# A conditioned decoder layer: loads in program order, scale and norm in one operation, remainder from the first part, quarter sums later

## The chip, the core and the metric

The kernel runs on one NeuronCore of a Trainium2 chip. The metric is the device time of one execution in microseconds, which is to be small. The core has a matrix engine (TensorE, PE in the profile; its weight loads are PEld), a vector engine (VectorE, DVE), an activation engine (ScalarE, ACT), GpSimd (POOL) and SyncE (SP), which here only issues transfers. Each runs its own instructions in order and waits on semaphores for the others. Transfers (DMA) are issued from the queues of SP, ACT and POOL.

## What is computed

One decoder layer over 2048 tokens of width 1024, and a final norm. Cut to what matters here:

```python
mod = c @ w_ada + b_ada                       # adaLN: shift, scale, gate
shift, scale, gate = split(mod, 3)
h = rmsnorm(x, g_pre) * (1.0 + scale) + shift
p = h @ w_in                                  # eight blocks of 1024 columns
y_a = conformer_conv_branch(p[A value], p[A glu], p[A silu], ...)   # conv of width 31
v = layernorm(gelu(p[B v]))                   # v: the block that the kernel takes first
s = tril(w_s) v + b_s                         # per head, in chunks of 128 positions
y_b = (gelu(p[B u]) * s * silu(p[B silu])) @ w_out_b
x = x + gate * ((sigmoid(p[gA]) * y_a + sigmoid(p[gB]) * y_b) @ w_o)
out = rmsnorm(x, g_final)
```

## The kernel before

All matrices are fp32. For the matrix engine each operand is split into two parts of type fp32r: the first part (`hi`) is a rounded copy made by ScalarE, the remainder (`lo`) is the value minus that copy. A product of two split operands is three matmuls: hi·hi, hi·lo and lo·hi. `split` (L84) does this for weights: ScalarE copies (L87), VectorE or GpSimd subtracts (L88).

The tokens are worked in two stages of 1024 (`s` = 0, 1), and a stage in two halves of 512. A stage first makes h, transposed: eight tiles `xn[k]` of 128 channels, of which `A[h][k]` are the split copies. Then it makes the v block (`first`, `v_pass`), its Gelu and layer norm (`v_half`, `v_norm`), and the position mixing per head (`mixing`, whose results `r` are stored to memory by GpSimd's queue). Then 28 steps called `quad` follow: each makes a 2x2 block product with seven products in place of eight, out of quarter sums `S1` to `S4` of h and sums of weight quarters. The convolution runs on VectorE beside them as background work. The output projections follow.

The change concerns the stretch before the first `quad` of stage 0, and in a smaller part the first `quad` of each stage:

- **The opening.** The first half of `xt` (x transposed) is loaded (L471), squared on ScalarE (L491, L494) and summed on VectorE (L495). `col_sums` and `spread` turn that into `rx`, the reciprocal norm of each token on all partitions. The row of c (`crow`) is loaded and spread over the partitions by two matmuls into `cbc` (L483, L486).
- **The first pass** is a loop of eight steps over k (L527). A step makes the adaLN columns of channel tile k + 1 (`ada`, L398: two reductions of 128x1024 weights `wa` against `cbc`, then an addition), scales `xn` by `rx` (`scaled`, L503), makes h twice on ScalarE by the Identity of scale times value plus shift (`shifted`, L507, through `modulated`, L364: once into the first part, once in place), and subtracts them for the remainder (L529). It splits two weight pieces of `w_v` by `prep_to` (L538). The matrix engine does 24 matmuls a step: 16 with the first part of h (L552, L553), 8 with the remainder (L557). The last step (L562 on) goes by output tile, so that tiles can be evicted one by one.
- **The norm of the second half** is taken from the second half of `xn`: squares (L545) in steps 4 to 7, sums (L560), `col_sums`, then `spread` and `make_h` (L369).
- **The quarter sums** (`halves_sums`, L378) are made for stage 0 and 1 at L633, and split into `S1` at once, into `S2`, `S4` and `S3` after the layer norm of the second half (`after`, L648).

The order within an engine is that of the program text inside `tc.manual_schedule(engines=MANUAL)` (L475), where MANUAL is PE, DVE, ACT and POOL. SP is not in it: a scheduler orders its loads, there and everywhere else, and all engines after the block. Pools bound how far a load may run ahead: 8 tiles `raw` for weights as loaded, 5 tiles `whl` for split pieces, 28 tiles `hs` for h, adaLN weights, v and sums, 6 small tiles `t512` (`r`, `rx` and others), 6 banks of PSUM.

## Time and profile before

| | us |
|---|---|
| median of the runs before (3 runs) | 1917.8 |
| lowest and highest run | 1916.1 and 1923.04 |
| the profiled execution | 1916.63 |
| its span in the trace | 1914.7 |

The profile page of that execution gives the matrix engine 96% busy, VectorE 70%, ACT 45% and POOL 46%. Of its forty slices of the span, the first, of some 48 us, has PE at 60%, the second at 70%, the third at 90% and nearly all others at 80% or more. A busy PE counts the modelled length of its matmuls, and the clock that it was granted is a figure of its own (1.00 is full speed, 2.4 GHz; 0.50 is 1.2 GHz). Times inside the trace run from the start of the span. Of a row of the timeline the first number is the start, the second the length; a count xN means N instructions merged into one row; in brackets stands how long the engine sat idle before, and who ended that.

### The profile page before, as it was taken

Reading aid. Unit: us, or ns where it says so; the run is one execution under the profiler, and the core shown is the slowest. Engines: PE = TensorE matmul, PEld = TensorE weight load, DVE = VectorE, ACT = ScalarE, POOL = GpSimd, SP = SyncE. Lnnn points to the kernel's source line nnn. Section 1 sums busy time; section 2 is a strip of 40 time slices with the busy share of each in tenths; the row PEclk is TensorE's granted clock in tenths of the full one; section 3 lists DMA queues with packets and bytes.
Section 4 is the critical chain, followed back from the end, with each engine's and each line's share of the span. In section 5 each row is a group of like instructions: output and inputs, shape, how many; then the busy total and the mean of one; then the engine's idle time right before and its main releaser. Section 6 shows DMA issues by size and latency. Waiting matters only on the chain.

```text
span 1914.7 us, 23225 instructions
## 1 busy us (share of the span) xinstructions
PE 1846.7 (96%) x8116; PEld 1507.4 (79%) x8116; DVE 1332.7 (70%) x1636; ACT 862.5 (45%) x1394; POOL 873.8 (46%) x734
## 2 busy tenths in 40 slices
PE   6798999999999999989999989999999998999998
PEld 4577888888888778778888878888888887888886
DVE  6775988888988874365851578789887798634424
ACT  4545555555455662312611454545554556512102
POOL 0035777777777740100100477777777776110000
PEclk9799999999999999999999999999999999999999
DMA  9562332223332368775886331333222333954494
GB/s 332 182 242 94 105 116 94 94 83 116 105 116 83 108 246 283 250 262 189 339 309 215 125 138 67 115 105 116 100 100 74 113 121 113 344 181 138 131 341 171
DMA packets 139015, 313.66 MB, mean 164 GB/s; under 512 B 15889, under 2 KB 16017, under 8 KB 138898
## 3 DMA queue, kind: packets, MB, share of 16 engines
q1 hardware_dynamic: 108434, 237.03, 36.5%
q0 software_dynamic: 11888, 41.43, 5.6%
q10 hardware_dynamic: 18576, 33.73, 4.6%
q8 instruction: 63, 1.03, 0.2%
q14 instruction: 54, 0.44, 0.1%
HBM read 226.66 MB, written 85.46 MB: 163 GB/s over the span
## 4 chain that ended last, share of the span: by engine, by line
PE 75%; issue 9%; DVE 6%; DMA 5%; ACT 3%; POOL 2%; SPq 0%; ACTq 0%; POOLq 0%; DVEq 0%
PE bank L297 21%; PE bank L303 21%; PE bank L300 21%; PE bank L312 3%; PE bank L313 3%; PE bank L314 3%; DVE a L892 1%; DMA raw<-in_wgate 1%; DVE wa L400 1%; PE bank L439 1%; DMA wa<-in_wada 1%; POOL whl L88 1%; DMA xn<-in_xt 1%; DMA whl<-d_wo 1%; ACT whl L87 1%
## 5 line engine op out<-in xcount | busy, mean ns | idle before, releaser
L88 POOL TENSOR_TENSOR whl<-raw,whl 128x512 fp32r<-128x512 f32 x392 | 520.9, 1333 | 348.5 <-ACT whl L87 344.0
L717 DVE SCALAR_TENSOR_TENSOR cv<-a,vec,cv 128x1024 f32<-128x1024 f32 x464 | 596.6, 1286 | 31.6 <-ACT cv L711 21.4
L87 ACT ACTIVATE whl<-raw 128x512 fp32r<-128x512 f32 x504 | 314.1, 626 | 405.8 <-PE bank L303 221.6
L300 PE MATMUL bank<-s,whl 128*128 128x512 f32 x896 | 350.2, 391 | 3.0 <-DVE s L88 3.0
L303 PE MATMUL bank<-s,whl 128*128 128x512 f32 x896 | 351.6, 392 | 0.0
L297 PE MATMUL bank<-s,whl 128*128 128x512 f32 x896 | 350.9, 392 | 0.0
L224 POOL TENSOR_TENSOR raw<-raw 128x512 f32<-128x512 f32 x224 | 295.8, 1321 | 17.2
L297 PE MATMUL bank<-h,whl 128*128 128x512 f32 x672 | 264.0, 393 | 0.5 <-DVE snap L693 0.4
L300 PE MATMUL bank<-h,whl 128*128 128x512 f32 x672 | 262.5, 391 | 0.0
L303 PE MATMUL bank<-h,whl 128*128 128x512 f32 x672 | 261.6, 389 | 0.0
L300 PEld LDWEIGHTS bank<-s,whl 128*128 128x128 f32 x896 | 168.9, 188 | 40.7 <-DVE s L88 5.1
L297 PEld LDWEIGHTS bank<-s,whl 128*128 128x128 f32 x896 | 169.0, 189 | 36.1 <-issue 1.2
L303 PEld LDWEIGHTS bank<-s,whl 128*128 128x128 f32 x896 | 169.0, 189 | 35.4 <-issue 0.8
L297 PEld LDWEIGHTS bank<-h,whl 128*128 128x128 f32 x672 | 126.1, 188 | 33.2 <-DVE snap L693 6.6
L303 PEld LDWEIGHTS bank<-h,whl 128*128 128x128 f32 x672 | 126.1, 188 | 26.8 <-issue 0.5
L300 PEld LDWEIGHTS bank<-h,whl 128*128 128x128 f32 x672 | 126.2, 188 | 26.0 <-issue 0.5
L88 DVE TENSOR_TENSOR whl<-raw,whl 128x512 fp32r<-128x512 f32 x112 | 76.0, 688 | 52.0 <-ACT whl L87 49.5
L921 POOL DMA_DIRECT2D mb<-gl x32 | 17.3, 541 | 201.3 <-DVE gl L920 201.3
L665 ACT ACTIVATE snap<-bank 128x512 f32<-128x512 f32 x112 | 66.5, 597 | 90.8 <-PE bank L303 90.8
L303 PE MATMUL bank<-ya,whl 128*128 128x512 f32 x256 | 100.6, 393 | 6.7 <-DVE whl L88 6.6
L297 PE MATMUL bank<-ya,whl 128*128 128x512 f32 x256 | 100.4, 392 | 0.5 <-ACT whl L87 0.5
L297 PE MATMUL bank<-yb,whl 128*128 128x512 f32 x256 | 99.8, 390 | 0.9 <-ACT whl L87 0.9
(218 smaller groups left out, 2882.2 us busy)
## 6 DMA issues: line engine op xcount, KB each, us to landing
raw<-in_w_in SPq DMA_DIRECT2D x224, 256.0 KB, 3.0
yb<-yb SPq DMA_DIRECT2D x32, 512.0 KB, 7.8
whl<-d_wo SPq DMA_DIRECT2D x32, 512.0 KB, 4.3
whl<-d_wv SPq DMA_DIRECT2D x32, 512.0 KB, 4.2
xn<-in_xt SPq DMA_DIRECT2D x32, 256.0 KB, 5.5
wa<-in_wada SPq DMA_DIRECT2D x16, 512.0 KB, 6.5
raw<-in_w_v SPq DMA_DIRECT2D x32, 256.0 KB, 4.8
d_wv<-whl POOLq DMA_DIRECT2D x16, 512.0 KB, 6.3
```

Of the source, the lines that this page charges most:

```text
L87: nc.scalar.activation(hi, val, AF.Copy)
L88: eng.tensor_tensor(out=lo, in0=val, in1=hi.bitcast(F32), op=ALU.subtract)
L224: eng.tensor_tensor(out=dst, in0=dst, in1=src, op=ALU.add)
L297: nc.tensor.matmul(pt, wh, h[:, 0], start=start and k == 0, stop=False, skip_group_check=True)
L300: nc.tensor.matmul(pt, wh, h[:, 1], start=False, stop=False, skip_group_check=True)
L303: nc.tensor.matmul(pt, wl, h[:, 0], start=False, stop=k == last, skip_group_check=True)
L312: nc.tensor.matmul(pt, xh, w[:, 0], start=kt == 0, stop=False)
L313: nc.tensor.matmul(pt, xh, w[:, 1], start=False, stop=False)
L314: nc.tensor.matmul(pt, xl, w[:, 0], start=False, stop=kt == KT - 1)
L400: nc.vector.tensor_tensor_reduce(out=wa[i], in0=wa[i], in1=cbc, scale=col(V_GPRE, k) if i else 1.0, scalar=0.0, op0=ALU.mult, op1=ALU.add, ...
L665: nc.scalar.activation(t, pt, AF.Copy)
L717: nc.vector.scalar_tensor_tensor(out=dst, in0=a[:, k : k + S], scalar=col(V_CW, j * TAPS + k), in1=cv[0], op0=ALU.mult, op1=ALU.add,)
```

## The change

1. SP joins the manual schedule of the block. The first half of `xn` is loaded by two queues, even tiles on SP and odd ones on ACT. `vec` (the small columns) is loaded by ACT behind them, not first. `cbc` is loaded by a transfer that repeats the row of c over the partitions; `crow`, its two matmuls and its two copies go. Then come the loads of step 0 to 3 (`load_step`: two `wa`, two `raw` each), and in step k those of step k + 4. In step 3 four tiles `sx` of x itself (tokens on partitions) and the second half of `xn` are queued behind them.
2. A small Sqrt (`warm`) is the first work on ACT, and a small Gelu comes before the evictions.
3. `scaled` multiplies by rx and by the adaLN scale in one operation (scalar_tensor_tensor). ScalarE then only adds the shift: `h_hi` into the first part, `shifted` in place. The remainder `h_lo` is (value + shift) minus the first part, in one VectorE operation, and so no longer reads what `shifted` writes.
4. The order in a step: `ada`, `scaled`, `h_hi`, the split of two weight pieces, `h_lo`, `shifted`.
5. The norm of the second half comes from `sx`: four Squares with accumulation on ScalarE, in steps 5 and 6, in place of eight Squares and four sums. Its `spread` stands between tile 2 and tile 3 of the last step.
6. The quarter sums are made later: S1 after the layer norm of the second half, S2, S4 and S3 with `mixing(1)`, which itself moves in the first `quad` from behind the third product to ahead of it.

```diff
-    def spread(cols, pt=None):
+    def diagonal(cols):
...
+        return diag
+
+    def spread(cols, pt=None, diag=None):
+        diag = diagonal(cols) if diag is None else diag
...
-    def modulated(dst, src, k):
+    def scaled(xn, rx, h, k):
+        v = xn[k][:, h * T : (h + 1) * T]
+        nc.vector.scalar_tensor_tensor(
+            out=v, in0=v, scalar=mod[:, k, 1:2], in1=rx, op0=ALU.mult, op1=ALU.mult
+        )
+
+    def shifted(xn, h, k, dst=None):
+        v = xn[k][:, h * T : (h + 1) * T]
         nc.scalar.activation(
-            dst, src, AF.Identity, bias=mod[:, k, 0:1], scale=mod[:, k, 1:2]
+            v if dst is None else dst, v, AF.Identity, bias=mod[:, k, 0:1]
         )
 
+    def h_hi(xn, h, k, A):
+        A[h].append(hs("h"))
+        shifted(xn, h, k, A[h][k][:, 0])
+
+    def h_lo(xn, h, k, A):
+        t = A[h][k]
+        nc.vector.scalar_tensor_tensor(
+            out=t[:, 1], in0=xn[k][:, h * T : (h + 1) * T], scalar=mod[:, k, 0:1],
+            in1=t[:, 0].bitcast(F32), op0=ALU.add, op1=ALU.subtract,
+        )
...
-    with tc.manual_schedule(engines=MANUAL):
...
+    with tc.manual_schedule(engines=MANUAL | {ET.SP}):
+        warm = sm.tile([P, 8], F32, tag="cols", name="warm")[:, :1]
+        nc.scalar.activation(warm, eps_t, AF.Sqrt)
+        for k in range(KT):
+            (nc.scalar if k % 2 else nc.sync).dma_start(
+                out=xn[k][:, :T], in_=xt[k * P : (k + 1) * P, :T]
             )
-            nc.scalar.activation(cbc[:, n * T : (n + 1) * T], pt, AF.Copy)
+        nc.scalar.dma_start(out=vec, in_=vecs)
+        nc.sync.dma_start(out=cbc, in_=rows[:, 3 * D : 4 * D].broadcast_to([P, D]))
+
+        def load_step(k):
+            wa[k] = load_ada(k)
+            for n in range(2):
+                raw_row(w_v, k, n)
+
+        for k in range(4):
+            load_step(k)
...
         for k in range(KT):
...
+            if k + 4 < KT:
+                load_step(k + 4)
+            if k == 3:
+                for c in range(NC):
+                    sx.append(hs32("sx"))
+                    nc.sync.dma_start(out=sx[c], in_=x[T + c * P : T + (c + 1) * P, :])
+                load_xn(0, 1, xn)
             if k + 1 < KT:
-                wa[k + 1] = load_ada(k + 1)
-                scaled(k + 1)
                 ada(k + 1, wa[k + 1])
+                scaled(xn, rx, 0, k + 1)
+                h_hi(xn, 0, k + 1, A)
                 prep_to(2 * k + 4)
-                shifted(k + 1)
-            if k == 2:
-                load_xn(0, 1, xn)
-            if k >= 4:
-                sq.append(hs32("q"))
-                for i in range(2):
+                h_lo(xn, 0, k + 1, A)
+                shifted(xn, 0, k + 1)
+            if k in (5, 6):
+                for c in (2 * k - 10, 2 * k - 9):
                     nc.scalar.activation(
-                        sq[-1][:, i * T : (i + 1) * T], xn[2 * (k - 4) + i][:, T:S], AF.Square
+                        sx[c], sx[c], AF.Square, accum_out=ssx[:, c : c + 1]
                     )
...
+        c1 = rstd_cols(ssx, NC)
+        diag1 = diagonal(c1)
+        nc.scalar.activation(warm, eps_t, AF.Gelu)
...
-            if u < 2:
-                evict(u)
...
+            if u == 2:
+                evict(0)
+                evict(1)
+                nc.scalar.activation(rx1, spread(c1, None, diag1), AF.Copy)
+                scaled(xn, rx1, 1, 0)
...
-        sums4 = [halves_sums(xn, k) for k in range(KH)]
...
+        S1 = sum_group(sum1)
+        S2, S4, S3 = [], [], []
+
+        def mix_second():
+            mixing(1, vn1, wsT, sbias)
+            S2.extend(sum_group(sum2))
+            S4.extend(sum_group(sum4))
+            S3.extend(sum_group(sum3))
...
             run_bg(2)
+            if beside:
+                beside.pop()()
             c = bank()
             prod(c, [take()], S1)
...
-            if beside:
-                beside.pop()()
             prod(c, [take()], S4, start=False)
```

Three places show how the order on the engines moves. The first is VectorE in one step of the first pass (`whl` are the weight pieces, `h` the split copy of h, `ISA` the two reductions and the reading of their sums). Before:

```order
L404 TENSOR_TENSOR mod<-mod,base 128x2
L88 TENSOR_TENSOR whl<-raw,whl 128x512 x2
L529 TENSOR_TENSOR h<-xn,h 128x512
L505 TENSOR_TENSOR xn<-xn,rx 128x512
L400 ISA wa,mod<-wa,cbc 128x1024
```

VectorE in one step after the change:

```order
L439 TENSOR_TENSOR mod<-mod,base 128x2
L374 SCALAR_TENSOR_TENSOR xn<-xn,mod,rx 128x512
L88 TENSOR_TENSOR whl<-raw,whl 128x512 x2
L390 SCALAR_TENSOR_TENSOR h<-xn,mod,h 128x512
L434 ISA wa,mod<-wa,cbc 128x1024
```

The scaling has moved from ahead of the reductions to behind them, directly ahead of the two subtractions for the weights.

ACT in two steps before, from the end of step 0's preparation on (L87 copies weight pieces, L365 makes h):

```order
L87 ACTIVATE whl<-raw 128x512 x4
L365 ACTIVATE h<-xn,mod 128x512
L365 ACTIVATE xn<-xn,mod 128x512
L87 ACTIVATE whl<-raw 128x512 x2
L365 ACTIVATE h<-xn,mod 128x512
```

ACT at the same place after the change:

```order
L380 ACTIVATE xn<-xn,mod 128x512
L380 ACTIVATE h<-xn,mod 128x512
L87 ACTIVATE whl<-raw 128x512 x2
L380 ACTIVATE xn<-xn,mod 128x512
L380 ACTIVATE h<-xn,mod 128x512
```

Before, four weight pieces were copied ahead of the second h, so that the copies ran one step ahead of the subtractions; now the two copies of a step stand behind that step's h.

The second place is SP's queue of loads at the start. Before:

```order
L469 DMA crow<-in_rows 1x1024
L342 DMA xn<-in_xt 128x512 x8
L394 DMA wa<-in_wada 128x1024 x2
L174 DMA raw<-in_w_v 128x512 x8
L342 DMA xn<-in_xt 128x512 x7
L394 DMA wa<-in_wada 128x1024 x2
L342 DMA xn<-in_xt 128x512
L174 DMA raw<-in_w_v 128x512 x2
L580 DMA wsT<-in_wst 128x1024
L394 DMA wa<-in_wada 128x1024 x2
```

SP's queue after the change, from the same start (six more pairs of each kind follow up to step 7):

```order
L515 DMA xn<-in_xt 128x512 x4
L519 DMA cbc<-in_rows 128x1024
L429 DMA wa<-in_wada 128x1024 x2
L177 DMA raw<-in_w_v 128x512 x2
L429 DMA wa<-in_wada 128x1024 x2
L177 DMA raw<-in_w_v 128x512 x2
```

The second half of `xn` and `wsT` have moved from ahead of the adaLN weights of step 1 and 2 to behind all of step 7.

The third place is PE in the first `quad` of stage 0, around `mixing(1)` (rows with `vn`). Before:

```order
L297 MATMUL bank<-s_1249,whl 128x512
L300 MATMUL bank<-s_1249,whl 128x512
L303 MATMUL bank<-s_1249,whl 128x512
L439 MATMUL bank<-wsT,vn 128x128 x28
L297 MATMUL bank<-s_1253,whl 128x512
L300 MATMUL bank<-s_1253,whl 128x512
L439 MATMUL bank<-wsT,vn 128x128 x4
```

PE there after the change:

```order
L305 MATMUL bank<-h,whl 128x512
L308 MATMUL bank<-h,whl 128x512
L311 MATMUL bank<-h,whl 128x512
L478 MATMUL bank<-wsT,vn 128x128 x32
L305 MATMUL bank<-s,whl 128x512
L308 MATMUL bank<-s,whl 128x512
L311 MATMUL bank<-s,whl 128x512
```

The 32 matmuls of the mixing have moved from behind the products with S1 and S2 to directly behind the two products with h, 24 matmuls into the `quad`.

## Rows read from the trace of the kernel before

**Rows 1.** Stretches: us, busy PE, PEld, DVE, ACT, POOL (instructions), clock, DMA.

```profile
0.00:22.47 22.47, 7.66 (x15) 3.45 (x15) 9.41 (x21) 11.27 (x18) 0.79 (x6) 1.00 0.89 316
22.47:74.80 52.33, 43.40 (x169) 33.78 (x169) 39.19 (x68) 22.13 (x36) 3.75 (x5) 0.93 0.74 265
74.80:87.66 12.86, 10.59 (x35) 7.34 (x35) 10.43 (x16) 8.89 (x14) 1.06 (x2) 0.76 0.45 142
87.66:148.33 60.67, 56.48 (x260) 45.32 (x261) 45.66 (x81) 31.75 (x51) 19.46 (x27) 0.94 0.59 221
148.33:183.00 34.67, 29.47 (x152) 24.02 (x150) 24.05 (x50) 16.53 (x29) 17.96 (x19) 0.95 0.30 107
183.00:600.00 417.00, 417.00 (x1836) 343.96 (x1836) 347.72 (x330) 223.89 (x352) 309.62 (x242) 1.00 0.30 100
```

**Rows 2.** Waits of PE in the first 260 us: total, times, longest.

```profile
PE bank L552 <- ACT h L365: 4.9, 1, 4.9
PE bank L565 <- ACT h L365: 3.9, 1, 3.9
```

**Rows 3.** Timeline, SP and DVE ahead of step 6 of the first pass.

```profile
53.16 0.90 SPq L394 DMA_DIRECT2D wa<-in_wada  x2
...
59.46 1.23 DVE L400 CUSTOM_DVE_ANT_0 wa<-wa,cbc 128x1024 f32<-128x1024 f32 x1 [4.89 <-DMA wa<-in_wada]
```

**Rows 4.** Timeline of the opening: spread, scaling, first h, first matmul.

```profile
16.80 2.04 PE L161 MATMUL bank<-diag,ones 128*128 128x512 f32 x2 [1.45 <-DVE diag L154]
...
19.51 0.69 DVE L505 TENSOR_TENSOR xn<-xn,bank 128x512 f32<-128x512 f32 x1 [0.31 <-ACT rx L500]
20.24 0.81 ACT L365 ACTIVATE h<-xn,mod 128x512 fp32r<-128x512 f32 x1 [0.76 <-DVE xn L505]
...
22.47 0.80 PE L552 MATMUL bank<-whl,h 128*128 128x512 f32 x1 [3.62 <-ACT whl L87]
```

**Rows 5.** Timeline of one step of the first pass, DVE and ACT.

```profile
36.55 0.69 DVE L529 TENSOR_TENSOR h<-xn,h 128x512 fp32r<-128x512 f32 x1 [0.53 <-ACT xn L365]
...
37.16 0.68 DVE L505 TENSOR_TENSOR xn<-xn,rx 128x512 f32<-128x512 f32 x1
...
40.23 0.16 DVE L404 TENSOR_TENSOR mod<-mod,base 128x2 f32<-128x2 f32 x1
...
41.27 0.82 ACT L365 ACTIVATE xn<-xn,mod 128x512 f32<-128x512 f32 x1
...
42.00 1.14 ACT L87 ACTIVATE whl<-raw 128x512 fp32r<-128x512 f32 x2
...
42.12 0.69 DVE L529 TENSOR_TENSOR h<-xn,h 128x512 fp32r<-128x512 f32 x1 [0.54 <-ACT xn L365]
```

**Rows 6.** Timeline: two matmuls at the low clock, and a table load.

```profile
64.10 0.63 PE L552 MATMUL bank<-whl,h 128*128 128x512 f32 x1
...
64.53 0.63 PE L553 MATMUL bank<-whl,h 128*128 128x512 f32 x1
...
88.47 1.28 ACT L524 ACT_TABLE_LOAD   x1
```

**Rows 7.** Groups by line: a weight copy, a Square of 1024, its sum's reading.

```profile
L87 ACT ACTIVATE whl<-raw 128x512 fp32r<-128x512 f32 x504 | 314.1, 626 | 405.8 <-PE bank L303 221.6 <-POOL raw L224 101.0 <-PE bank L314 62.0
...
L1007 ACT ACTIVATE junk<-xo 128x1024 bf16<-128x1024 f32 x12 | 12.6, 1047 | 68.1 <-DVE xo L991 67.9 <-ACT junk L1007 0.2
L1007 ACT ACTIVATION_READ_ACCUMULATOR junk<-xo 128x1 f32 x12 | 2.2, 186 | 0.0
```

**Rows 8.** Timeline of the first quads: DVE and PE of stage 0, PE of stage 1.

```profile
151.51 3.95 DVE L412 TENSOR_SCALAR vn<-vn,mv,rs 128x1024 f32<-128x1024 f32 x4
...
169.31 0.75 DVE L445 SCALAR_TENSOR_TENSOR r<-bank,vec,sbias 128x512 f32<-128x512 f32 x1 [6.06 <-DMA r<-r]
...
170.11 2.08 PE L439 MATMUL bank<-wsT,vn 128*128 128x128 f32 x8 [3.61 <-DVE r L445]
...
1106.91 1.16 PE L439 MATMUL bank<-wsT,vn 128*128 128x128 f32 x8 [3.69 <-DVE r L445]
```

More of the change, by code (lines that the diff above doesn't have):

```diff
@@ L176, in raw, with raw_row @@
         return t
+    def raw_row(mat, k, n):
+        raw(mat, (id(mat), k, n), mat[k * P : (k + 1) * P, n * T : (n + 1) * T])
     def piece_tile():
@@ L183, in prep @@
             w = piece_tile()
-            split(w, raw(mat, None, mat[k * P : (k + 1) * P, n * T : (n + 1) * T]))
+            if (id(mat), k, n) not in raws:
+                raw_row(mat, k, n)
+            split(w, raws.pop((id(mat), k, n)))
             if cache:
@@ L390, in load_ada, with sum4, sum3 @@
+    def sum4(xn, k):
+        a11, a12, a21, a22 = quarters(xn, k)
+        nc.vector.tensor_tensor(out=a12, in0=a12, in1=a11, op=ALU.add)
+        return a12
+    def sum3(xn, k):
+        return quarters(xn, k)[2]
     def load_ada(k):
@@ L557, in hybrid_layer @@
                     nc.tensor.matmul(first[u], xl, ws[n][:, 0], start=False, stop=False)
[L558 to L561 removed]
+        c1 = rstd_cols(ssx, NC)
+        diag1 = diagonal(c1)
+        nc.scalar.activation(warm, eps_t, AF.Gelu)
+        rx1 = t512("rx1")
         for u in range(2 * NC):
@@ L607, in hybrid_layer @@
             vn0, st0 = vn_first, st_first
-            for k in range(1, KT):
+            for k in range(2, KT):
                 make_h(xn, rx1, 1, k, A)
+            for k in range(2):
+                shifted(xn, 1, k)
         else:
```

143 lines of the change are left out of this document (60 added, 83 removed).

## The prediction, made before the changed kernel ran

> **What bounds the kernel now.** I read the stretches first [rows 1]. From 183 to 600 us PE is busy without a gap at clock 1.00: 1836 records in 417 us, or 0.227 us a matmul, so nothing can be gained there by this change. All that is slack lies ahead: the opening (no product until 22.47), the first seven steps of the first pass (52.33 us), its last step with the turn to the second half (12.86), the second half's passes (60.67) and the first `quad` of stage 0 (34.67). At 0.227 us the 24 matmuls of a step want 5.45, seven steps 38.1; they took 14.2 more.
>
> Next I asked who PE waited for. Two waits stand out, 4.9 and 3.9 us, both for ScalarE's h [rows 2]. The timeline shows that ScalarE was not the cause: VectorE sat 4.89 us until adaLN weights landed, which SP had issued only 6.3 us before it began [rows 3]. The scheduler had put the second half of `xn` and other loads ahead of them. After such a pause the matmuls come 0.43 us apart, that is 1.2 GHz, for some microseconds [rows 6]. So the loads are late in steps 6 and 7, and the clock is paid on top. In the steps without a late load, VectorE comes round every 5.57 us (36.55 to 42.12) [rows 5]: nearly PE's own 5.45.
>
> **The change part by part**, against the profiled execution (1916.63 us; the median of the runs is 1.2 above).
>
> *1. Loads, opening and steps.* With step k + 4 loaded in step k, every load of a step has three steps, some 19 us, to land; the rows of before show 6.3 [rows 3]. I take the load waits as gone. But the step itself becomes longer. In the new order VectorE goes: scale, two weight subtractions, remainder, two reductions, addition. The weight copies that the subtractions need stand on ScalarE behind the h, which needs the scale. VectorE therefore waits for ScalarE once in each step. The period, link by link:
> - scale to start of h: 0.73 (19.51 to 20.24) [rows 4].
> - start of h to start of the copy behind it: a copy frees the engine after 0.52 (two in 1.14, the last 0.63 long), today's Identity with two column operands after 0.73 (41.27 to 42.00) [rows 5, 7]. The new one has one such operand; I take the middle, 0.63.
> - copy to the first subtraction: 0.65, from its 626 ns [rows 7].
> - two subtractions until the remainder starts: 2 times 0.61 (36.55 to 37.16 is one operation of this size) [rows 5].
> - remainder to the addition: 3.07, as from 37.16 to 40.23, one operation of that size and the two reductions [rows 5].
> - addition to scale: 0.20.
>
> The sum is 6.50 (bounds 6.39 and 6.60). That is 0.93 more than before and 1.05 more than PE wants, so PE pauses about a microsecond in each step.
>
> The opening: up to the spread (16.80 to 18.84) [rows 4] I leave times as they are, since the last tile of `xn` decides and the same bytes come first. Before, two Identities and a copy lay between the scaling at 19.51 and the first matmul at 22.47. Now the copies are done while the spread runs, VectorE has its second reduction and two subtractions behind the diagonal done by about 19.3, and only scaling and one Identity remain: 19.3 + 0.73 + 0.73 = 20.8. The remainder starts there, the addition 3.07 later, the scaling of step 1 at 24.1. Six periods on, step 7's scaling is at 24.1 + 39.0 = 63.1, and its first matmul 0.73 + 0.63 + 0.63 later, at 65.1. Before it was at 74.80 [rows 1]. **Gain 9.7**; by the period's bounds 9.1 to 10.4, and 2 either way for the opening.
>
> In the trace of before all of these loads run on one queue, at 316 GB/s up to 22.47 [rows 1], so no row shows two queues sharing. The Trainium skill ("DMA: Bandwidth & Descriptors", "Queues, rings and completion order") says that each DMA engine takes turns between the queue rows that have work. By it the odd `xn` tiles on ACT's queue share with `cbc` and the first `wa` on SP's, 1 MB, 3.3 us at that rate, and the total would be 3 us higher than mine.
>
> *2. The last step.* It costs something that was hidden. On ScalarE behind h(7) stand five weight copies, the in-place shift, two Squares of `sx` (1.05 and 0.19 for the sum each) [rows 7] and the Sqrt. By these lengths the reciprocal starts 7.7 us after the scaling and the diagonal is ready at 8.6. PE has its first nine matmuls done at about 5.6, as the third waits for the remainder, and in its order the spread comes next: it waits 3.0 us. I expect the low clock then, as before behind the 3.9 wait [rows 2]: spread 2.04 [rows 4], five matmuls at 0.43, ten at 0.227, so the second half starts 15.0 after the scaling, 13.0 after the step's first matmul. Before: 12.86. **Gain 0**, bounds 2 either way. What goes (four sums, a matmul of sums, two of three table loads of 1.28 [rows 6]) pays for the pause.
>
> *3. The second half's passes.* Their work is the same. 60.67 us at a mean clock of 0.94 [rows 1] lost 3.6 us to the low clock, and the first row waited about 1 us for h and Gelu. Both belong to the late turn and should go. Moving the quarter sums off VectorE should help, but some twenty operations for norms and remainders still stand ahead of the weight subtraction that PE wants in the fourth row; by 0.61 each I find that it still waits some 2 us there. **Gain 3.8**, bounds 0 and 7.
>
> *4. The first `quad` of stage 0.* It idled 5.2 us (34.67 less 29.47) and lost 1.7 to clock 0.95 [rows 1]. The longest wait is 3.61 for `r`, and behind it VectorE waited 6.06 for the store of an earlier `r` [rows 8], which stood on GpSimd's queue behind four of its operations. The new order on GpSimd has two of its operations ahead of the first store, one ahead of the second and none between the next two. In exchange the mixing stands 24 matmuls into the `quad`, 5.4 us, while the normed v is ready 7.1 us into it (151.51 + 3.95 against 148.33) [rows 1, 8]; less three short matmuls, PE waits 1.1. **Gain 5.6**, bounds 1 (the wait for the store stays) and 7.
>
> *5. The first `quad` of stage 1* has the same wait, 3.69 [rows 8]. Less the 1.1: **gain 2.6**, bounds 0 and 4.
>
> Operations that only change form (one scalar_tensor_tensor for one tensor_tensor, a Square of 1024 for two of 512) I take at equal cost per element. From 183 on PE hides VectorE and ScalarE.
>
> Sum: 9.7 + 0 + 3.8 + 5.6 + 2.6 = 21.7. 1916.63 - 21.7 = 1894.9, and 1.2 up for the median: **1896**.
>
> **The rivals.**
> - *The step is not lengthened* (the copies start earlier than I read): 5.57 as before, six times 0.93 more gain, 1890. For it: only one wait makes the difference. Against: the order on both engines. 0.08.
> - *The pauses bring the low clock back in the steps.* A step whose first four microseconds run at half speed takes 24 x 0.227 + 9 x 0.2 = 7.3; then PE has no pause, and the clock rises. 0.8 to 0.9 a step, seven steps: 1902. 0.10.
> - *The gain behind the first pass doesn't come* (terms 3 to 5 are waits that only move): 1896 + 12 = 1908. For it: ScalarE and VectorE have no less to do in these stretches. 0.11.
> - *The change doesn't do what it says*, since SP's queue runs in order and a load that waits for a free tile holds up those behind it: step 7 begins as late as before, and the pauses stay. 1917. Against: a `raw` of step k + 4 waits for a subtraction of step k, three steps ahead of need. 0.04.
> - *Slower: the low clock holds through the whole first pass.* The place is PE's pause in each step. At 0.43 a step takes 10.3, 3.8 more than mine; seven steps and 3.8 in the last give 30.4, 1926. It eats the whole gain from the sixth such step on. Without terms 3 to 5 it is 1938. Against: 10.3 leaves no pause, and before the clock rose in the middle of step 0 and of step 6. 0.05. The Trainium skill ("TensorE: Matmul & The Clock Gate", "A second HAM failure mode: psum-queue depth-cycling") has a kernel in which short idles between groups of matmuls made the clock swing. In this trace pauses of a quarter to half a microsecond in each step left it at 1.00; no row has a microsecond in every step.
>
> **How the numbers follow.** My case has 0.62, with a range of its own from 1888 to 1903 (terms 3 to 5 set it). The range that should hold 8 in 10 goes from 1886, some 2 us under the first rival with a better opening, to 1910, over the third rival. 0.5%, about what a measurement of this kernel can tell from no change, is 9.6 us: faster is below 1908.2, slower above 1927.4. Faster: 0.62 + 0.08 + 0.10 and half of the 0.11, which sits on the edge, 0.85. Same: the other half, 0.04, and 0.02 of the slower rival, 0.12. Slower: 0.03.
>
> **What would show it.** Steps 2 to 6: VectorE's remainder every 6.5 us, with a wait of about 1.4 for the copies and none for loads; PE idle near 1 us a step at clock 1.00. Step 7 starting near 65, second half near 78, first `quad` near 135. In the last step a pause of about 3 us ahead of the spread. In both first `quad`s no wait for a store of `r`, and about 1 us for the normed v. The prediction is wrong if loads still end VectorE's waits, if a step takes 5.6 or 10, or if the first `quad` keeps a wait over 3 us.

## The result, and the profile after

| | before | changed |
|---|---|---|
| median of the runs, us (4 and 4) | 1918.28 | 1898.33 |
| lowest and highest run, us | 1916.10 and 1923.04 | 1895.41 and 1903.82 |
| profiled execution and its span, us | 1916.63, 1914.7 | 1895.41, 1893.7 |

The ratio of the runs is 0.9896, with a 95% interval of 0.9864 to 0.9928: about 20 us faster, and clear of no change. Forecast were 1896, a range of 1886 to 1910, and for the profiled execution 1894.9.

The stretches of the changed kernel, cut at the same places as [rows 1] (first matmul, step 7, second half, first `quad`); the columns are those of [rows 1]:

```profile
0.00:20.66 20.66, 3.91 (x10) 2.28 (x10) 10.68 (x23) 8.27 (x15) 0.79 (x6) 1.00 0.89 324
20.66:65.75 45.09, 43.09 (x169) 32.13 (x169) 35.35 (x62) 19.48 (x33) 1.78 (x2) 1.00 0.92 345
65.75:78.71 12.96, 8.63 (x26) 5.59 (x27) 9.12 (x16) 11.21 (x21) 1.60 (x3) 0.87 0.74 264
78.71:136.32 57.61, 53.61 (x261) 43.66 (x260) 50.45 (x88) 31.40 (x54) 22.44 (x29) 1.00 0.63 229
```

The seven steps took 45.09 us in place of 52.33, at a mean clock of 1.00 in place of 0.93, and moved 345 GB/s in place of 265. (The clock column leaves out the slow start: in both kernels the first pass begins with matmuls that come 0.43 us apart, eight of them here and six before.) The last step kept its length (12.96 for 12.86). The second half's passes took 57.61 for 60.67. The waits of PE in the first 260 us, as in [rows 2] (above these stands only the opening's wait for the sum of squares):

```profile
...
PE bank L164 <- ACT vn L562: 3.3, 1, 3.3
PE bank L592 <- ACT h L380: 1.9, 1, 1.9
PE bank L321 <- DVE whl L88: 1.6, 1, 1.6
...
PE bank L305 <- ACT bank L719: 1.1, 1, 1.1
PE bank L320 <- ACT vn L460: 1.0, 1, 1.0
PE bank L593 <- DVE whl L88: 0.9, 4, 0.2
PE bank L592 <- ACT whl L87: 0.9, 4, 0.2
```

The two long waits for a late h are gone; the 1.9 is the opening. What is left in the steps is eight waits of 0.2, all for weight copies or subtractions. They understate the pause, because the profile gives a matmul a length of 0.39 us while the next starts 0.227 us behind it. By the starts of the matmuls, steps 1 and 2, which began late behind the slow start, took 5.44 and 5.82 us, and from step 3 on, at 39.34, a step took 6.60: four pauses of 1.15 (6.60 less PE's 5.45) up to step 7. The new long one is that of the spread, 3.3, and its releaser is an eviction. One step of the first pass on VectorE and ScalarE, to be read against [rows 5]:

```profile
30.65 0.75 DVE L374 SCALAR_TENSOR_TENSOR xn<-xn,mod,rx 128x512 f32<-128x512 f32 x1
31.44 0.72 ACT L380 ACTIVATE h<-xn,mod 128x512 fp32r<-128x512 f32 x1 [2.55 <-DVE xn L374]
32.07 1.14 ACT L87 ACTIVATE whl<-raw 128x512 fp32r<-128x512 f32 x2
32.72 1.29 DVE L88 TENSOR_TENSOR whl<-raw,whl 128x512 fp32r<-128x512 f32 x2 [1.31 <-ACT whl L87]
33.93 0.75 DVE L390 SCALAR_TENSOR_TENSOR h<-xn,mod,h 128x512 fp32r<-128x512 f32 x1
...
37.06 0.16 DVE L439 TENSOR_TENSOR mod<-mod,base 128x2 f32<-128x2 f32 x1
37.26 0.75 DVE L374 SCALAR_TENSOR_TENSOR xn<-xn,mod,rx 128x512 f32<-128x512 f32 x1
...
39.32 1.29 DVE L88 TENSOR_TENSOR whl<-raw,whl 128x512 fp32r<-128x512 f32 x2 [1.31 <-ACT whl L87]
```

No load ends a wait of VectorE any more. It waits 1.31 us in each step, for a copy that stands behind h on ScalarE, and comes round every 6.60 us (32.72 to 39.32). The links of the chain are 0.79, 0.63, 0.65, 1.21, 3.13 and 0.20; the prediction had 0.73, 0.63, 0.65, 1.22, 3.07 and 0.20.

The gain at the first `quad` reaches into the second, so it is measured over the first two: from the first product of the first `quad` to the first product of the third. In the changed kernel (two rows of stage 0, then two of stage 1):

```profile
136.32 0.39 PE L305 MATMUL bank<-h,whl 128*128 128x512 f32 x1
...
180.53 0.39 PE L305 MATMUL bank<-h,whl 128*128 128x512 f32 x1
...
1067.35 0.39 PE L305 MATMUL bank<-h,whl 128*128 128x512 f32 x1
...
1111.07 0.39 PE L305 MATMUL bank<-h,whl 128*128 128x512 f32 x1
```

and where the third `quad` begins in the kernel before:

```profile
199.03 0.39 PE L297 MATMUL bank<-h,whl 128*128 128x512 f32 x1
...
1134.11 0.39 PE L297 MATMUL bank<-h,whl 128*128 128x512 f32 x1
```

Stage 0 took 44.21 us in place of 50.70 (199.03 less 148.33), stage 1 43.72 in place of 49.04 (1134.11 less 1085.07, where its first `quad` starts in the trace of before).

### The profile page after: what moved, and what is told of

Read it like the earlier page. It is cut to its first block, busy times and chain, and to the rows that moved or that the text cites. A ratio compares the mean times of both kernels' runs of the same rounds, so it can differ in the third digit from the quotient of the medians.

```text
span 1893.7 us, 23201 instructions
## 1 busy us (share of the span) xinstructions
PE 1837.6 (97%) x8104; PEld 1502.4 (79%) x8104; DVE 1326.2 (70%) x1608; ACT 854.5 (45%) x1392; POOL 876.0 (46%) x734
## 4 chain that ended last, share of the span: by engine, by line
PE 75%; issue 9%; DMA 6%; DVE 4%; ACT 2%; POOL 2%; SPq 0%; ACTq 0%; POOLq 0%; DVEq 0%
PE bank L305 22%; PE bank L311 22%; PE bank L308 22%; PE bank L320 3%; PE bank L322 3%; PE bank L321 3%; DMA raw<-in_w_v 1%; PE bank L478 1%; DMA wo<-d_wo 1%; DVE a L941 1%; DMA raw<-in_wgate 1%; ACT whl L87 1%; DMA xn<-in_xt 1%; DVE rsq L895 1%; POOL whl L88 1%
## 5 line engine op out<-in xcount | busy, mean ns | idle before, releaser
L87 ACT ACTIVATE whl<-raw 128x512 fp32r<-128x512 f32 x504 | 314.7, 627 | 389.2 <-PE bank L311 224.5
```

The costliest lines, as they stand in the source:

```text
L87: nc.scalar.activation(hi, val, AF.Copy)
```

## The experiments

Thirteen kernels have a trace beside the one before. This table has the start of six places in each, in us from the start of the span, and the times; the names are those of the experiments below. The kernel before ran again with each group of experiments, and its median was 1918.27 to 1920.33.

| | first matmul | step 7 | second half | first quad, stage 0 | third quad, stage 0 | first quad, stage 1 | median, us | ratio to before (95%) |
|---|---|---|---|---|---|---|---|---|
| before | 22.47 | 74.80 | 87.66 | 148.33 | 199.03 | 1085.07 | 1918.28 | |
| changed | 20.66 | 65.75 | 78.71 | 136.32 | 180.53 | 1067.35 | 1898.33 | 0.9896 (0.9864, 0.9928) |
| b_load | 22.64 | 63.18 | 75.37 | 136.89 | 187.39 | 1072.05 | 1904.96 | 0.9930 (0.9904, 0.9956) |
| b_sums | 22.49 | 74.93 | 87.87 | 149.91 | 193.71 | 1078.28 | 1905.69 | 0.9932 (0.9917, 0.9946) |
| b_load_sums | 22.41 | 63.09 | 75.11 | 136.87 | 180.68 | 1069.53 | 1895.74 | 0.9867 (0.9846, 0.9888) |
| copies_ahead | 20.96 | 61.81 | 73.78 | 131.40 | 175.61 | 1068.28 | 1892.89 | 0.9866 (0.9845, 0.9886) |
| pause | 19.89 | 73.13 | 86.34 | 144.70 | 188.92 | 1078.41 | 1906.59 | 0.9934 (0.9915, 0.9952) |
| norm_earlier | 20.56 | 65.63 | 73.62 | 136.34 | 180.16 | 1066.74 | 1897.26 | 0.9885 (0.9861, 0.9909) |
| mix_late | 20.79 | 66.28 | 79.42 | 137.58 | 182.64 | 1072.62 | 1902.75 | 0.9912 (0.9893, 0.9931) |
| one_queue | 19.80 | 64.87 | 78.08 | 135.77 | 179.98 | 1067.95 | 1896.70 | 0.9877 (0.9859, 0.9895) |
| both | 20.45 | 61.02 | 67.34 | 128.63 | 172.43 | 1061.50 | 1888.61 | 0.9844 (0.9829, 0.9860) |
| pool_v | 20.12 | 60.79 | 67.11 | 135.84 | 179.64 | 1066.42 | 1897.81 | 0.9887 (0.9871, 0.9902) |
| weights_between | 20.76 | 60.30 | 66.61 | 120.63 | 167.55 | 1059.39 | 1884.55 | 0.9819 (0.9793, 0.9845) |
| all_four | 19.92 | 60.30 | 66.61 | 120.56 | 167.99 | 1059.26 | 1886.67 | 0.9816 (0.9802, 0.9829) |

Executions of one kernel differ by up to 9 us. The traces differ by some 8 us between the third `quad` of stage 0 and the first of stage 1, where these kernels are nearly alike (the last section). So stages are compared by the places in the table, and the median is the second witness. Even the places spread: the eight kernels that open as the changed one does have their first matmul between 19.89 and 20.96.

### Is it the lateness of the loads? b_load

```diff
-    with tc.manual_schedule(engines=MANUAL):
+    with tc.manual_schedule(engines=MANUAL | {ET.SP}):
+        load_xn(0, 0, xn)
+        for k in range(4):
+            load_step(k)
...
+            if k + 4 < KT:
+                load_step(k + 4)
+            if k == 3:
+                load_xn(0, 1, xn)
```

> The kernel before with the new order of loads alone: SP in the manual schedule, the adaLN weights and weight pieces of step 0 to 3 first, those of step k + 4 in step k, the second half of xn behind step 7. The order on the other engines in a step is the old one. Theory (late loads alone cost the first pass its time, and the old step of about 5.5 us has no pause): the waits of 4.9 and 3.9 us for h go, step 7 starts at 61 to 63 in place of 74.80, and the time is 11 to 13 us below the kernel before, as much in these steps as the whole change brings or more. Rival (old Squares of the second half's xn, which now lands last, hold ScalarE up in steps 4 to 6): PE waits for h again by 3 us or more, and the gain is 5 to 8 us.

The theory held; its numbers were passed a little. The median fell by 14.5 us (forecast 11 to 13). Step 7 starts at 63.18 (forecast 61 to 63), and the seven steps take 40.54 us, 4.55 less than in the changed kernel. PE's waits of 4.9 and 3.9 for h are not there; the longest in the first 55 us behind the first matmul is 1.6:

```profile
PE bank L317 <- ACT h L370: 1.6, 1, 1.6
PE bank L581 <- DVE h L542: 0.8, 1, 0.8
```

So the order of loads alone brings the first pass more than the whole change does, and the new order within a step gives a part of it back.

### Is it the later quarter sums? b_sums

```diff
-        sums4 = [halves_sums(xn, k) for k in range(KH)]
...
-        S2, S4, S3 = rest
+        S1 = sum_group(sum1)
+        def mix_second():
+            mixing(1, vn1, wsT, sbias)
+            S2.extend(sum_group(sum2))
...
+            if beside:
+                beside.pop()()
             c = bank()
             prod(c, [take()], S1)
```

> The kernel before with its quarter sums made as in the changed kernel (S1 behind the layer norm, the rest with the second mixing) and the mixing ahead of the product with S1; nothing else. Theory (the two first quads gained 6.5 and 5.3 us by this part alone): the first quad of stage 0 takes about 33.5 us in place of 39.8 and that of stage 1 about 33 in place of 38.1, and the time is 10 to 12 us below the kernel before. Rival (stage 0's part needs the earlier turn of the first pass): stage 1 gains 5, stage 0 less than 2, and the time is 5 to 7 us below.

The theory held, and the median fell by more than forecast, 13.7. From the first to the third `quad` stage 0 took 43.80 us (149.91 to 193.71) and stage 1 43.72 (1078.28 to 1122.00), 6.9 and 5.3 less than before. It needs nothing of the earlier stages. Of the 6.9 in stage 0, 5.3 arrive at the third `quad` (199.03 less 193.71), mostly because the second half's passes took 62.04 us in place of 60.67: moving the sums is not free there.

### Place of the mixing, or place of the sums? mix_late

```diff
         def mix_second():
-            mixing(1, vn1, wsT, sbias)
...
+            if late:
+                mixing(*late.pop())
             prod(c, [take()], S4, start=False)
```

> The changed kernel with the second mixing put back to its old place in the first quad, between the products with S2 and S4; the quarter sums stay where the change put them. Theory (the place of the mixing is what took the waits away): PE waits for r again, about 3 us in the first quad of each stage, and the time is 4 to 7 us above the changed kernel. Rival (it was the later sums on VectorE that did it): no wait over 1.5 us for r in either quad, and the time is within 2 us of the changed kernel.

The time, 4.4 above the changed kernel, is the theory's; the mechanism is not. The waits of PE in stage 0's first two `quad`s hold no r:

```profile
PE bank L308 <- DVE s L88: 1.1, 1, 1.1
PE bank L305 <- ACT bank L719: 0.4, 1, 0.4
PE bank L305 <- ACT s L87: 0.2, 1, 0.2
```

(In the kernel before the mixing stood there behind the fourth product, the one with S2.) The two stretches took 45.06 us (137.58 to 182.64) and 45.08 (1072.62 to 1117.70 in its trace), 0.85 and 1.36 more than in the changed kernel. That is 2.2 of the 11.8 gained there; the rest of the 4.4 lies where nothing was edited. So it is the sums' move that removed the wait, by at least 9.6 us, and the mixing's move adds up to 2.2.

The traces show how. In the kernel before, ScalarE copied seven sums as soon as the layer norm was done, and loaded a table behind them; the weight copy that GpSimd needed came after that. GpSimd sat idle for 7.64 us, then did four operations, and only then issued the first stores of `r`:

```profile
155.56 3.76 ACT L87 ACTIVATE s<-xn 128x512 fp32r<-128x512 f32 x7 [3.19 <-DVE s L92]
...
161.82 1.27 POOL L88 TENSOR_TENSOR whl<-raw,whl 128x512 fp32r<-128x512 f32 x1 [7.64 <-ACT whl L87]
...
166.83 1.63 POOL L454 DMA_DIRECT2D r<-r  x3
```

In mix_late as many operations of GpSimd stand ahead of these stores, but it was not held up:

```profile
145.77 1.28 POOL L88 TENSOR_TENSOR whl<-raw,whl 128x512 fp32r<-128x512 f32 x1 [1.85 <-ACT whl L87]
...
152.05 1.63 POOL L493 DMA_DIRECT2D r<-r  x3
```

From the start of the first `r` on VectorE to its store it took 6.1 us before (160.71 to 166.83) and 1.8 here (150.22 to 152.05).

### What does the new order in a step cost? copies_ahead and pause

```diff
-                h_hi(xn, 0, k + 1, A)
                 prep_to(2 * k + 4)
+                h_hi(xn, 0, k + 1, A)
```

> The changed kernel with one line moved: in a step of the first pass the two weight copies on ScalarE stand ahead of h, not behind it. VectorE's order is the same. Theory (the copies behind h are what lengthens the step): VectorE no longer waits 1.31 us for the copies, the period falls from 6.60 to about 5.6, PE's pauses in the steps go, step 7's first matmul comes at about 59.5 in place of 65.75, and the time is 6 to 7 us below the changed kernel, some 27 below the kernel before. Rival (the loads set the pace: the DMA engines are 0.92 busy at 345 GB/s from 20.66 to 65.75): VectorE's wait for copies becomes a wait for adaLN weights in the later steps, the period stays above 6.2, and the gain is 0 to 2 us.

VectorE's wait is gone; the same place of a step:

```profile
39.94 0.75 DVE L374 SCALAR_TENSOR_TENSOR xn<-xn,mod,rx 128x512 f32<-128x512 f32 x1
40.02 0.63 ACT L87 ACTIVATE whl<-raw 128x512 fp32r<-128x512 f32 x1 [1.38 <-PE cv L597]
40.61 1.28 DVE L88 TENSOR_TENSOR whl<-raw,whl 128x512 fp32r<-128x512 f32 x2
40.73 0.73 ACT L380 ACTIVATE h<-xn,mod 128x512 fp32r<-128x512 f32 x1
...
45.14 0.75 DVE L374 SCALAR_TENSOR_TENSOR xn<-xn,mod,rx 128x512 f32<-128x512 f32 x1
```

VectorE comes round every 5.20 us (39.94 to 45.14), faster than in the kernel before (5.57) and than PE's own 5.45, and now ScalarE's copy waits for PE to free a weight tile: PE is the bound. PE is busy without a gap from 20.96 to 61.81, 40.85 us in place of 45.09, and the median is 5.4 lower. The loads do not bind, although they then move 386 GB/s. The gain of 5.4 is less than the 6 to 7 forecast, which had step 7 at 59.5 (it started at 61.81): the forecast had left out the slow first matmuls of the pass, of which this trace has twelve. The opposite edit puts two copies more into the same chain:

```diff
                 h_hi(xn, 0, k + 1, A)
+                for _ in range(2):
+                    nc.scalar.activation(t512("q"), rx, AF.Copy)
```

> The changed kernel with two more copies of 128x512 on ScalarE between h and the weight copies of each step (work that is not needed): PE's pause in a step grows from about 1 us to about 2. Theory (the period is the chain scale, h, copy, subtractions, remainder, reductions, and such pauses leave the clock alone): the period goes from 6.60 to about 7.65, the matmuls of steps 2 to 6 stay at 0.227 us, and the time is 7 us above the changed kernel. Rival (pauses bring the low clock): matmuls at 0.43 us show in each step; where they fill the whole of it a step takes 10.3 us and the time is 20 us or more above the changed kernel, where they fill a part the period stays at 7.65 and the rows alone show it.

The period is 7.64 (one is 8.53: there a reduction took 2.17 us beside an operation of GpSimd), and the median is 8.3 above the changed kernel, as the theory has it. But the clock was not left alone. Three stretches, up to step 4, step 4, and steps 5 and 6, with the granted clock third from the end:

```profile
22.00:49.31 27.31, 23.13 (x92) 17.03 (x91) 17.56 (x32) 12.92 (x23) 0.00 (x0) 1.00 0.88 330
49.31:56.95 7.64, 7.41 (x24) 5.49 (x24) 5.22 (x10) 3.53 (x7) 0.00 (x0) 0.78 1.04 401
56.95:73.13 16.18, 12.44 (x51) 8.70 (x49) 11.35 (x19) 9.14 (x17) 1.78 (x2) 1.00 0.47 174
```

After a pause of 1.5 us and two of 2.2 (7.64 less 5.45) step 4 ran partly at the low clock, eight matmuls from 50.64 on 0.43 us apart. VectorE's period stayed 7.64, since the slow matmuls only filled the pause. Step 7 fell to the low clock too, behind a pause of 2.2 and a short wait of its own; steps 2, 3 and 6, behind pauses of 1.5, 2.2 and 2.9, did not. So the rival of the low clock is real at pauses of this size, though not each time, and cost nothing in the steps; behind the changed kernel's four pauses of 1.15 the clock stayed at 1.00. What decides between the two is not shown.

### Can the pause of the last step be won? norm_earlier, both

```diff
-            if k in (5, 6):
-                for c in (2 * k - 10, 2 * k - 9):
+            if k in (4, 5):
+                for c in (2 * k - 8, 2 * k - 7):
...
                 h_lo(xn, 0, k + 1, A)
+                if k == 6:
+                    c1 = rstd_cols(ssx, NC)
+                    diag1 = diagonal(c1)
+                    nc.scalar.activation(warm, eps_t, AF.Gelu)
                 shifted(xn, 0, k + 1)
```

> The changed kernel with the second half's norm one step earlier: the four Squares in steps 4 and 5 in place of 5 and 6; root, reciprocal, diagonal and the small Gelu inside the preparation of step 7, ahead of its in-place shift. Theory (the pause ahead of the spread is ScalarE's queue in the last step): the 3.35 us wait of the spread falls below 0.5, the low clock behind it goes, the second half starts about 8.5 us after step 7's first matmul in place of 12.96, and the time is 4 to 5 us below the changed kernel. Rival (VectorE bounds the second half's passes, 50.45 us busy of 57.61): the second half starts earlier, but its fourth row waits as much longer (1.6 becomes 5 to 6), and the time is within 1 us of the changed kernel.

The rival held (the median is 1.1 below the changed kernel's, at the edge of its 1). The spread no longer waits, the second half starts 7.99 us behind step 7 in place of 12.96, and the first `quad` starts where it did, at 136.34 for 136.32. The fourth row took it all (a row is the twelve matmuls of one channel tile of `w_v`; the fourth is the first whose weights VectorE splits behind the h of all the tiles):

```profile
PE bank L321 <- DVE whl L88: 6.4, 1, 6.4
PE bank L608 <- DVE h L390: 0.8, 1, 0.8
```

With the copies ahead as well (both edits, diffs as above):

> The changed kernel with the weight copies ahead of h in each step and the second half's norm one step earlier. Theory (VectorE's queue sets when the fourth row of the second half can start, so what is won at the spread comes back there): the second half starts near 69, its fourth row waits about 6 us, and the time is that of the kernel with the copies alone, 1892 to 1894. Rival (that wait came from weight pieces which had been ordered another way, not from VectorE's work): the wait stays below 3 us, and the time is 1888 or less.

Neither as it was put. The wait is the theory's, 5.3, but with it the first `quad` starts at 128.63, 2.8 earlier than with the copies alone, and the median is 1888.6: the gain at the spread came back in part only.

### VectorE's work, or its order? pool_v and weights_between

```diff
-            split(w, raws.pop((id(mat), k, n)))
+            split(w, raws.pop((id(mat), k, n)), nc.gpsimd if cache is d_wv else nc.vector)
```

> The kernel with both edits (copies ahead, norm earlier), and the sixteen weight subtractions of the second half's passes on GpSimd in place of VectorE. Theory (the fourth row waits for VectorE's queue): GpSimd needs 1.34 us for one, PE takes one piece in 2.7, so the fourth row waits less than 1 us, the first quad starts near 126 in place of 136.32, and the time is 5 to 6 us below the kernel with both edits, about 1887. Rival (GpSimd's work holds VectorE up, as one reduction took 2.17 us in place of 1.28 beside an operation of GpSimd): VectorE's operations take longer by as much as it gives away, the wait goes to the norms and remainders, and the gain is 0 to 2 us.

The direction is the rival's, and its size was missed: 9.2 us slower than both edits, not 0 to 2 faster. Three scalings beside GpSimd's subtractions, and three after them:

```profile
70.87 4.12 DVE L374 SCALAR_TENSOR_TENSOR xn<-xn,mod,rx 128x512 f32<-128x512 f32 x3
71.13 3.32 POOL L88 TENSOR_TENSOR whl<-raw,whl 128x512 fp32r<-128x512 f32 x2 [1.19 <-ACT whl L87]
...
78.60 2.07 DVE L374 SCALAR_TENSOR_TENSOR xn<-xn,mod,rx 128x512 f32<-128x512 f32 x3
...
89.47 6.87 DVE L451 TENSOR_SCALAR vn<-vn,mv,rs 128x1024 f32<-128x1024 f32 x4
```

The same three took 4.12 us beside GpSimd and 2.07 without it, and the four of the layer norm 6.87 in place of the 3.96 of the changed kernel. The fourth row's wait is gone, but PE waited 3.5 us for a remainder and 6.9 us in the mixing for the bias that VectorE made late. The Trainium skill ("SBUF — State Buffer", "SBUF: two separate sides") says that a VectorE operation with two inputs in SBUF and a GpSimd operation that reads it block each other for a whole instruction; the rows agree in the main: three scalings alone (2.07) and two subtractions of 1.27 make 4.6 us one after the other, and the five were done in 4.12. The layer norm's operations have one such input, so the sentence does not cover them; that they took longer is shown, why is not. So work on GpSimd is no relief for VectorE here. The other way leaves the work and changes the order:

```diff
             for k in range(2, KT):
                 make_h(xn, rx1, 1, k, A)
+                prep_to(18 + k)
```

> The kernel with both edits (copies ahead, norm earlier), and each weight piece of the second half's first rows split right behind the h of one channel tile, not behind all six. Nothing is taken off VectorE, its order alone changes. Theory (the fourth row waits because its subtraction stands behind some twenty operations, not because VectorE has too much to do): the 5.3 us wait of the fourth row falls below 1, no other wait over 1.5 takes its place, the first quad starts near 124 in place of 128.6, and the time is about 1884. Rival (VectorE has more to do than the rows of PE give it time for): the rows wait by 4 to 5 us in all at another place, for a remainder or a scaling, and the time stays within 2 us of 1888.6.

The theory held ahead of the `quad`. VectorE does as much as before (52.77 us busy in these passes, 53.06 with both edits), and PE has one wait from 60 to 130 us. It is a new one, behind the start of the `quad`, which the theory did not have:

```profile
PE bank L305 <- ACT bank L721: 2.5, 1, 2.5
```

The second half's passes take 54.02 us (66.61 to 120.63) in place of 61.29, at the gapless pace of PE. The first two `quad`s give a part back: 46.92 (120.63 to 167.55) in place of 43.80. With 1884.55 it beats both kernels: 35 us below the one before, 14 below the change.

### The opening, the sum of the parts, and the whole

```diff
-            (nc.scalar if k % 2 else nc.sync).dma_start(
+            nc.sync.dma_start(
```

> The changed kernel with all eight tiles of the first half of xn on SP's queue, ahead of cbc and the adaLN weights. Theory (the odd tiles on ACT's queue share the DMA engines with what SP has queued behind its four tiles): the last tile lands 1 to 2 us ahead of 12.00, the first matmul starts near 19.5 in place of 20.66, and the time is 1 us lower. By the page of the Trainium skill on turns between queue rows, and 1 MB at 324 GB/s, it would be 3 us. Rival (the adaLN weights of step 0 then land later and hold VectorE up): first matmul at 20.5 or later, no gain.

The first matmul comes at 19.80 in place of 20.66, and the last Square ends at 11.43 (8.75 and 2.68 for four) in place of 12.63, as the theory has it. But this is not clear of the spread: the eight kernels with two queues have their first matmul between 19.89 (pause, whose opening is that of the changed kernel) and 20.96, the two with one queue (this one and all_four) at 19.80 and 19.92. So two queues cost between nothing and about 1 us here, and not 3. The median, 1.6 lower, lies within the changed kernel's runs.

> The kernel before with the two parts together that were tried alone: the new order of loads, and the later quarter sums with the earlier mixing. The step, the opening and the second half's norm are the old ones. Theory (the parts touch different stretches and add up: 14.5 and 13.7): 28 us below the kernel before, 1891, so that the rest of the change costs about 7. Rival (they share a gain, as the whole change brings only 20): 19 to 22 below, 1898.

In between by the median, 24 below the kernel before. By the places it meets the changed kernel: its third `quad` starts at 180.68, that of the changed kernel at 180.53. What the rest of the change (opening, step, norm from x) wins it loses again: 1.8 in the opening and 4.1 in the second half's passes (57.61 for 61.76) against 4.4 in the steps (45.09 for 40.68), 0.9 in the last step (12.96 for 12.02) and 0.4 in the first two `quad`s (44.21 for 43.81).

> The changed kernel with all four edits: copies ahead of h, norm one step earlier, weight pieces between the h of the second half, and the first half of xn on SP's queue alone. Theory (each edit has its own stretch): first matmul near 19.8, second half near 65.7, first quad of stage 0 near 119.7, and the time 1 us below the 1884.6 of the kernel without the fourth edit, 1883 to 1884, 35 to 36 below the kernel before. Rival (what is won ahead of the first quad is given back between the quads of the two stages, where 13 profiles so far show 895 to 904 us): first quad as said, but 1885 to 1889.

The median is the rival's, but it does not decide: the runs go from 1882.03 to 1887.77, and those of the kernel without the fourth edit from 1882.49 to 1891.66. The two cannot be told apart, and no gain of the fourth edit is shown. The places were nobody's: the second half starts at 66.61 and the first `quad` at 120.56, for 65.7 and 119.7 forecast. The 0.84 us won in the opening are gone by the second step, which begins at 27.66 with and without them, because PE stayed longer at the low clock. The last matmul at 0.43 us, and the first behind it, of this kernel:

```profile
23.93 0.63 PE L597 MATMUL bank<-whl,h 128*128 128x512 f32 x1
24.35 0.47 PE L596 MATMUL bank<-whl,h 128*128 128x512 f32 x1
```

and of the kernel without the fourth edit, which started at 20.76:

```profile
23.06 0.63 PE L597 MATMUL bank<-whl,h 128*128 128x512 f32 x1
23.48 0.46 PE L596 MATMUL bank<-whl,h 128*128 128x512 f32 x1
```

Ten matmuls against six. That is no rule: how many matmuls were slow at the start did not follow the time of the first one. pause began as early, at 19.89, with seven slow matmuls and its second step at 27.11; copies_ahead began at 20.96 with twelve and its second step at 29.17. Between the third `quad` and stage 1 it took 891.27 us, where the kernel before took 886.04; but the kernel without the fourth edit took 891.84, so this gives no difference between the two.

## Why the prediction was right, step by step

| term | gain forecast | gain measured | from |
|---|---|---|---|
| 1 loads, opening, steps | 9.7 | 9.05 | start of step 7, 74.80 to 65.75 |
| 2 last step | 0 | -0.1 | 12.86 to 12.96 |
| 3 second half's passes | 3.8 | 3.06 | 60.67 to 57.61 |
| 4 first two quads, stage 0 | 5.6 | 6.49 | 50.70 to 44.21 |
| 5 first two quads, stage 1 | 2.6 | 5.32 | 49.04 to 43.72 |
| elsewhere | 0 | -2.8 | the rest of the span's 21.0 |
| sum | 21.7 | 21.0 | 1914.7 to 1893.7 |

That the sum came within 0.7 us of the trace is in part luck: term 5 gave 2.7 more than forecast, and the rest of the kernel, which the forecast put at nothing, took 2.8 back.

- **Term 1** held link by link: first matmul 20.66 (20.8), scaling of step 1 at 24.05 (24.1), period 6.60 (6.50), step 7 at 65.75 (65.1). Both halves of its argument were then shown on their own: the loads by b_load (step 7 at 63.18 without the new order), the price of the new order by copies_ahead (4.2 us of steps) and pause.
- **Term 2** held in its sum, by luck. Its pause was 3.35 where 3.0 was forecast. The releaser was named wrong: the diagonal was done at 71.84, and the spread went at 72.96, when the eviction freed its bank. That eviction stood behind the one table load that was left (70.92 to 72.20), which the forecast had nowhere: it counts the two that go, and lets the spread wait for the diagonal alone. So the spread came 9.3 us behind the scaling (63.66), not 8.6; and 5.8 us later, not 6.4, the second half started, since fewer matmuls than forecast came at 0.43. The two misses cancel.

```profile
70.92 1.28 ACT L600 ACT_TABLE_LOAD   x1
71.15 0.69 DVE L150 TENSOR_TENSOR diag<-ident,cols 128x512 f32<-128x512 f32 x1
...
72.96 2.07 PE L164 MATMUL bank<-diag,ones 128*128 128x512 f32 x2 [3.35 <-ACT vn L562]
```

- **Term 3** was close: the clock went from 0.94 to 1.00, the waits of 0.5 and 0.4 for h and Gelu at the start went, and the fourth row's wait stayed (1.58, forecast 2; 2.0 before). What the forecast lacked are two new waits of 0.8 and 0.5 in the first mixing, for the bias and an `r`. norm_earlier, both and weights_between show that what is won ahead of the fourth row comes back there, wholly or in part, until VectorE's order is changed.
- **Term 4** was right in size for a reason that was half wrong. The prediction put the wait for r down to GpSimd's order of stores. mix_late has the first stores behind as many operations again, and no wait: GpSimd had been late because ScalarE's copies for the sums stood ahead of the weight copy that it needed. (Its own parts, 5.2 and 1.7 less 1.1, make 5.8, not the 5.6 put down.) The prediction also let the mixing's new place pay 1.1 for the normed v. That wait did not come; a wait of 1.1 did, but for ScalarE's copy (L719), which stood behind the layer norm's root and its table load. mix_late shows that the sums' move, not the mixing's, does most of it.
- **Term 5** was mis-sized by half. The forecast counted one wait of 3.69 less 1.1 for the normed v. The 1.1 did not come, and PE's 1.4 us of waits for the sums (L300 on VectorE's s, in the trace of before) went too, which the sum had left out. A longer wait for ScalarE's copy (L719, 0.7) came in return. From start to start of the matmuls, the wait for r cost 3.9 us and those for the sums 2.0; less 0.6 for the copy that is the 5.3.
- **Elsewhere** the trace of the changed kernel is 0.8 us longer between the two stages' first `quad`s and 2.0 behind stage 1's. Of the 0.8, 0.4 lie in stage 1's passes ahead of its first `quad`: they take 94.63 to 94.67 us in every kernel with the later sums, and 94.21 and 94.23 in b_load and the kernel before. The rest lies where nothing was edited, and one trace of each cannot tell it from the spread.

Of the rivals, the lengthened step was real, so the first is out. The low clock in the steps did not come behind pauses of 1.15; pause shows that it can behind pauses of 1.5 to 2.9. (The pauses of the kernel before, which the prediction gives as a quarter to half a microsecond, were 0.1 to 0.2 by the starts of steps 1 to 5, so they say less about this rival than it took from them.) The 3 us that two queues sharing would have cost did not come either: the first matmul was at 20.66, where 20.8 was forecast without them. That terms 3 to 5 only move waits was wrong here, though right for what norm_earlier won. The slower end would have needed every step at the low clock.

## What to carry to other kernels

Price an edit by the chain that decides there, link by link, and ask of every gain which queue it meets next: 5 us won at the spread were given back three rows on, and 8 came at the first `quad` once VectorE's order there was changed. When several parts are changed at once, try the parts alone: here two of them reach the gain of all, and what the others win in two places they lose in two more. Do not move work to a second engine before looking at how long the first one's operations take while the second is busy.

## What was not expected of the hardware

- One VectorE scaling (two inputs, L374 in pool_v) took up to 1786 ns beside GpSimd's subtractions, and 749 at the median.
- How long the first pass stayed at the low clock was different in each trace: of the ten kernels with the new opening, the fewest slow matmuls at the start are six (weights_between) and the most twelve (copies_ahead), with first matmuls 0.2 us apart (20.76 and 20.96). The second step begins 1.5 us apart in them (27.66 and 29.17). Why is not shown.
- The time from the third `quad` of stage 0 to the first of stage 1, in which the kernels are nearly alike, was 884.6 to 892.7 us in the 14 traces. The remaining `quad`s took 509.3 to 513.2 of it, the projections behind them 279.0 to 286.3, and stage 1's passes 94.2 to 94.7: most of the spread is in the projections. The last of them, from its first matmul to the first of stage 1's passes, in b_load and then in copies_ahead, whose longest wait of PE there is 2.6 us where b_load has one of 0.6 (the columns are those of [rows 1]):

```profile
887.71:977.83 90.12, 89.55 (x390) 72.91 (x389) 63.03 (x111) 35.95 (x55) 9.04 (x17) 1.00 0.90 326
```

```profile
879.89:973.64 93.75, 91.15 (x390) 74.10 (x389) 64.70 (x111) 34.18 (x55) 9.03 (x17) 0.98 0.86 313
```

The shortest are from kernels that arrive late (b_sums 884.6, b_load 884.7, before 886.0), the longest from kernels that arrive early (copies_ahead 892.7, weights_between 891.8, all_four 891.3); but pause arrives as late as b_load and took 889.5. Whether an early arrival costs time there, or it is the spread of single executions, one trace of each cannot tell; it stays open.
